# A Mamba scan moved one chunk ahead, and its decays moved to GpSimd

## The chip, the cores and the metric

One Trainium2 chip, one core. The metric is the device time of one execution in microseconds. The engines are TensorE (PE; its weight loads are PEld), VectorE (DVE), ScalarE (ACT), GpSimd (POOL) and SyncE (SP), whose queue issues nearly all DMAs. Each engine takes its instructions in a fixed order.

## The reference

Two layers over 2048 tokens of width 1024: a Mamba-2 mixer and a multi-head latent attention, each behind an RMS norm and with a residual add. The change is in the mixer. Cut to what matters there:

```
proj = h @ w_in;  z, xBC, dt_raw = split(proj)
xBC  = silu(causal_depthwise_conv(xBC, conv_w, conv_b));  xs, Bm, Cm = split(xBC)
dt   = softplus(dt_raw + dt_bias);  A = -exp(A_log)
# per chunk of the sequence, for each of 4 groups (8 heads of 64 channels each):
cum  = cumsum(dt * A)
L    = exp(where(causal, cum[t] - cum[s], -inf))
y    = (C_t . B_s) L dt_s x_s  summed over s
     + exp(cum[t]) C_t . state
state = state * exp(cum[-1]) + sum_s B_s exp(cum[-1] - cum[s]) dt_s x_s
y    = (y + D_skip * x) * silu(z);  y = rms(y over the group) * g_out;  h + y @ w_out
```

## The kernel before

The sequence is cut into four blocks of 512 tokens (`b`) and the mixer's channels into four groups (`g`); `mamba` walks over the sixteen pairs. While the scan of one pair runs, the projections of its neighbours run on TensorE: the output projection `outp` of the pair before, the convolved inputs `xbc` and the gate `zgate` of the next. Each projection is a sweep over k with four PSUM banks (tag `mm`), and each product is three matmuls of high and low halves (L403 to L405). At the end of a sweep the banks are emptied: `hs` on DVE (L1121), `craw` on ACT (L1056, followed by the convolution: L1060 on ACT, three L1062 on DVE, tanh L1064, L1065), `sz` on ACT and DVE (L1091, L1092). In block 0 and 1 the weights are split into halves on ACT and DVE as they come (L434, L437, L442); from block 2 on they are read back already split.

The scan is a Python generator, `ssd(b, g)`, that yields five times per chunk of 128 tokens, four chunks per pair, so 64 chunks in all. `mamba` advances it by one yield for every step or two of the projections; this sets where its instructions stand among theirs. A scheduler orders each engine's instructions by that order of issue, with some shifts where an operand is late. The steps of a chunk:

1. Fetch the chunk's cumulated decays, broadcast to all partitions, into `E` (128 x 8 x 128, tag `big`, two buffers; L1225); transpose B and form C.B on TensorE; split B and C into halves (`Bt`, `Ct`); mask (`CB`); on ACT eight times Relu with a bias per head (L1237) and one exponential (L1238); on DVE multiply by `CB` (L1239).
2. Transpose x (L1244); `Xd` = x dt and `y` = x D on DVE (L1247, L1250); `Xw` = x times the end weight, eight heads on ACT (L1253).
3. Split `Xw` into `Xp` (ACT L1208, POOL L1209); the products of `E` and `Xd` (L1260); the products of `Ct` and the state's halves `Sp` (L410 to L412); add both into `y`.
4. The products of `Bt` and `Xp` (L410 to L412); the state decays and takes them in (L1277, L1278); split the state into `Sp`.
5. Gate `y`, take its power, write it out transposed.

POOL's work in the mixer is the low halves of `Ct`, `Xp` and `Sp` (L1209) and small copies of the convolution's halo (L1055, L1057). `steps(b)` makes `dt`, the cumulated decays and the end weights once per block.

Of the kernel before, what the change touches and what calls it, by code (L numbers as in the profile page):

```python
# [26 lines left out]
G = 4  # L27
# [359 lines left out]
class Net:  # L387
# [492 lines left out]
    def mamba(self, cp):  # L880
        nc = self.nc
        self.state = [None] * G
        self.xn, self.xT, self.dtv, self.conv, self.sz, self.yT, self.rr, self.hs = {}, {}, {}, {}, {}, {}, {}, {}
# [6 lines left out]
        for n, (b, g) in enumerate(items):  # L890
# [34 lines left out]
            scan, done, step = self.ssd(b, g), 0, 0  # L925
# [202 lines left out]
    def steps(self, b):  # L1128
# [9 lines left out]
        wk = self.t(self.sp, "big", [P, D], bufs=2)  # L1138
# [7 lines left out]
        raw, e, q, p, dA, cT = (wk[:, n * P:n * P + P] for n in range(6))  # L1146
# [38 lines left out]
        v.tensor_tensor(wend, wend, dt, ALU.mult)  # L1185
# [6 lines left out]
    def ssd(self, b, g):  # L1192
# [3 lines left out]
        BT, CT, *xs = self.conv.pop((b, g))  # L1196
        szs = self.sz.pop((b, g))
# [3 lines left out]
        def v8(x):  # L1201
            return x.rearrange("p (h d) -> p h d", h=8)

        def pair(tag, n, bufs):
            return self.t(self.sp, tag, [P, 2, n], F32R, bufs=bufs)

        def halves(u, x):
            act(u[:, 0], x, AF.Copy)  # L1208
            nc.gpsimd.tensor_tensor(u[:, 1], x, u[:, 0].bitcast(F32), ALU.subtract)  # L1209
            return u  # L1210

        if b:
            old = halves(pair("Sp", TB, 1), self.state[g])
        for c in range(4):
            s = slice(c * P, (c + 1) * P)
            h0 = c * H + g * 8

            def heads(x):
# [5 lines left out]
            E = self.t(self.sp, "big", [P, D], bufs=2).rearrange("p (h t) -> p h t", h=8)  # L1224
            nc.sync.dma_start(E.rearrange("p h t -> p (h t)"),  # L1225
                              cumT[h0:h0 + 8, :].rearrange("h t -> (h t)").partition_broadcast(P))
            pb = self.t(self.pp, "tr", [P, TB], bufs=4)
            nc.tensor.transpose(pb[:, 0:P], BT[:, s], self.ident)
            nc.tensor.matmul(pb[:, P:2 * P], BT[:, s], CT[:, s], start=True, stop=True)
            Bt = pair("Bt", P, 2)  # L1230
            self.split(Bt[:, 0], Bt[:, 1], pb[:, 0:P])
            if not first:
                Ct = halves(pair("Ct", P, 2), CT[:, s])
            CB = self.t(self.sp, "CB", [P, P], bufs=2)
            v.tensor_tensor(CB, pb[:, P:2 * P], self.triu, ALU.mult)
            for h in range(8):
                act(E[:, h, :], E[:, h, :], AF.Relu, bias=ncum[:, h0 + h:h0 + h + 1])  # L1237
            act(E, E, AF.Exp, scale=-1.0)  # L1238
            v.tensor_tensor(E, E, CB.unsqueeze(1).to_broadcast([P, 8, P]), ALU.mult)  # L1239
            yield  # L1240

            px = self.t(self.pp, "tr", [P, TB], bufs=4)
            for j in range(4):
                nc.tensor.transpose(px[:, j * P:(j + 1) * P], xs[j][:, s], self.ident)  # L1244
            Xd, Xw = self.t(self.sp, "Xd", [P, TB], bufs=2), self.t(self.sp, "Xw", [P, TB], bufs=1)
            with self.tc.high_priority(20):
                v.tensor_tensor(v8(Xd), v8(px), heads(dt), ALU.mult)  # L1247
            y = self.t(self.sp, "y", [P, TB], bufs=2)
            skip = self.Dsk[:, g * 8:g * 8 + 8].unsqueeze(2).to_broadcast([P, 8, 64])
            v.tensor_tensor(v8(y), v8(px), skip, ALU.mult)  # L1250
            for h in range(8):
                hc = slice(h * 64, (h + 1) * 64)
                act(Xw[:, hc], px[:, hc], AF.Copy, scale=wend[:, h0 + h:h0 + h + 1])  # L1253
            yield
            Xp = halves(pair("Xp", TB, 1), Xw)
# [5 lines left out]
            v.tensor_tensor(y, y, yi, ALU.add)  # L1261
            if not first:
                pi = self.t(self.pp, "tr", [P, TB], bufs=4)
                self.late3(pi, Ct[:, 0], Ct[:, 1], old[:, 0], old[:, 1])
                t = self.t(self.sp, "yt", [P, TB], bufs=2)
                v.tensor_tensor(v8(t), v8(pi), heads(ecum), ALU.mult)
                v.tensor_tensor(y, y, t, ALU.add)
            yield
            if not last:
                pst = self.t(self.pp, "tr", [P, TB], bufs=4)  # L1270
                self.late3(pst, Bt[:, 0], Bt[:, 1], Xp[:, 0], Xp[:, 1])
                if first:
                    st = self.state[g] = self.t(self.sp, f"st{g}", [P, TB], bufs=1)
                    v.tensor_copy(st, pst)
                else:
                    st = self.state[g]
                    v.tensor_tensor(v8(st), v8(st), heads(dec), ALU.mult)  # L1277
                    v.tensor_tensor(st, st, pst, ALU.add)  # L1278
                if c < 3:
                    old = halves(pair("Sp", TB, 1), st)  # L1280
# [35 lines left out]
        self.rr[b, g] = rr  # L1316

# [668 lines left out]
```

## Time and profile before

| | |
|---|---|
| Median of 3 runs | 2924.01 us (2920.55 to 2924.09) |
| Profiled execution | 2919.59 us, span 2917.8 us |
| Busy over the span | PE 96%, PEld 56%, DVE 75%, ACT 64%, POOL 34% |
| Mean granted TensorE clock | 0.993 |
| DMA | 507.56 MB, mean 174 GB/s |

In the profile, a group of instructions is named by its line in the kernel, its engine, and out<-in by the names of the tiles. "PE tr L1260 <- DVE big L1239: 10.1, 6, 2.2" says that TensorE's instructions of line 1260 waited for DVE's of line 1239 that write `big`, 10.1 us in all, six times, 2.2 us at most. In a row of groups the last number is the idle time of the engine in front of these instructions, with what ended it. The ends of matmuls are modelled; what can be read of them is the distance between their starts.

### The profile page before, as it was taken

Reading aid. Unit: us, or ns where it says so; the run is one execution under the profiler, and the core shown is the slowest. Engines: PE = TensorE matmul, PEld = TensorE weight load, DVE = VectorE, ACT = ScalarE, POOL = GpSimd, SP = SyncE. Lnnn points to the kernel's source line nnn. Section 1 sums busy time; section 2 is a strip of 40 time slices with the busy share of each in tenths; the row PEclk is TensorE's granted clock in tenths of the full one; section 3 lists DMA queues with packets and bytes.
Section 4 is the critical chain, followed back from the end, with each engine's and each line's share of the span. In section 5 each row is a group of like instructions: output and inputs, shape, how many; then the busy total and the mean of one; then the engine's idle time right before and its main releaser. Section 6 shows DMA issues by size and latency. Waiting matters only on the chain.

```text
span 2917.8 us, 48835 instructions
## 1 busy us (share of the span) xinstructions
PE 2802.7 (96%) x16349; PEld 1648.5 (56%) x16349; DVE 2189.3 (75%) x4757; ACT 1854.4 (64%) x4731; POOL 985.2 (34%) x1200
## 2 busy tenths in 40 slices
PE   7999999998999999999999999999999999999898
PEld 6787755444444444444455455454555555555587
DVE  6778888888877777788776654544888898889476
ACT  7888777666666555666555343432888888888322
POOL 1211112212111221122111212222888888888400
PEclk9999999999999999999999999999999999999899
DMA  5343356665657544476544765556899999999884
GB/s 187 90 120 96 97 167 209 190 186 175 186 157 241 172 127 145 121 223 189 150 140 114 240 200 193 175 171 207 165 183 182 188 187 182 182 188 197 220 265 154
DMA packets 602144, 507.56 MB, mean 174 GB/s; under 512 B 413954, under 2 KB 455938, under 8 KB 601892
## 3 DMA queue, kind: packets, MB, share of 16 engines
q1 hardware_dynamic: 590020, 466.03, 61.3%
q0 software_dynamic: 11872, 38.41, 3.7%
q8 instruction: 128, 2.10, 0.3%
q14 instruction: 124, 1.02, 0.1%
HBM read 303.37 MB, written 104.47 MB: 140 GB/s over the span
## 4 chain that ended last, share of the span: by engine, by line
PE 64%; DVE 14%; ACT 7%; DMA 7%; issue 5%; POOL 2%; SPq 1%; ACTq 0%; POOLq 0%; DVEq 0%
PE mm L403 11%; PE mm L405 11%; PE mm L404 11%; PE tr L403 5%; PE tr L405 5%; PE tr L404 5%; PE mm L1758 4%; DVE cacc L1062 3%; DMA big<-cumT 2%; PE tr L1758 2%; PE mm L1731 2%; DMA wraw<-in_ssm_w_in_dram 2%; PE tr L1731 2%; PE tr L1260 2%; ACT big L1237 1%
## 5 line engine op out<-in xcount | busy, mean ns | idle before, releaser
L1723 POOL TENSOR_TENSOR HL<-Pr,HL 128x512 f16<-128x512 f32 x320 | 370.0, 1156 | 25.6
L403 PE MATMUL mm<-xT,wsp 128*128 128x512 f16 (+1 forms) x800 | 308.4, 385 | 7.4 <-DVE sz L1092 5.3
L404 PE MATMUL mm<-xT,wsp 128*128 128x512 f16 (+1 forms) x800 | 306.1, 383 | 0.0
L405 PE MATMUL mm<-xT,wsp 128*128 128x512 f16 (+1 forms) x800 | 305.2, 383 | 0.6 <-DVE wsp L434 0.5
L1209 POOL TENSOR_TENSOR Xp<-Xw,Xp 128x512 fp32r<-128x512 f32 x64 | 87.2, 1363 | 563.1 <-ACT Xp L1208 536.5
L403 PE MATMUL mm<-wsp,xT 128*128 128x512 f16 (+2 forms) x640 | 233.6, 366 | 1.9 <-ACT craw L1056 1.3
L404 PE MATMUL mm<-wsp,xT 128*128 128x512 f16 (+2 forms) x640 | 232.9, 364 | 1.0 <-DVE wsp L442 1.0
L1717 ACT ACTIVATE Pr<-tr,nm 128x512 f32<-128x512 f32 (+3 forms) x332 | 206.2, 626 | 41.8 <-DVE nm L1712 40.1
L405 PE MATMUL mm<-wsp,xT 128*128 128x512 f16 (+2 forms) x640 | 232.5, 364 | 0.0
L1062 DVE SCALAR_TENSOR_TENSOR cacc<-craw,pack,cacc 128x512 f32<-128x512 f32 x288 | 220.8, 785 | 11.9 <-ACT cacc L1060 10.2
L1722 POOL CAST HL<-Pr 128x512 f16<-128x512 f32 x320 | 195.0, 609 | 91.2 <-ACT Pr L1717 88.7
L1717 ACT ACTIVATE Pr<-mm,nm 128x512 f32<-128x512 f32 (+3 forms) x308 | 191.9, 628 | 44.5 <-DVE nm L1712 38.7
L1706 DVE TENSOR_REDUCE mx<-tr 128x1 f32<-128x512 f32 (+3 forms) x332 | 195.6, 602 | 28.3 <-PE tr L1682 25.9
L403 PE MATMUL mm<-wsp,yT 128*128 128x512 f16 (+1 forms) x512 | 199.4, 389 | 13.3 <-DVE hs L1121 7.2
L1237 ACT ACTIVATE big<-big,d_cum 128x128 f32<-128x128 f32 x512 | 169.8, 391 | 55.4 <-DMA big<-cumT 54.8
L1706 DVE TENSOR_REDUCE mx<-mm 128x1 f32<-128x512 f32 (+3 forms) x308 | 182.1, 604 | 27.6 <-PE mm L1682 20.6
L404 PE MATMUL mm<-wsp,yT 128*128 128x512 f16 (+1 forms) x512 | 197.7, 386 | 0.5 <-DVE wsp L442 0.5
L405 PE MATMUL mm<-wsp,yT 128*128 128x512 f16 (+1 forms) x512 | 197.4, 386 | 0.0
L405 PEld LDWEIGHTS <-xT 128*128 128x128 f16 (+1 forms) x1280 | 124.5, 97 | 117.2 <-issue 2.6
L403 PEld LDWEIGHTS <-xT 128*128 128x128 f16 (+1 forms) x1280 | 125.0, 98 | 106.1 <-issue 14.4
L1253 ACT ACTIVATE Xw<-tr,d_wend 128x64 f32<-128x64 f32 x512 | 111.7, 327 | 111.7 <-DVE y L1250 99.4
L404 PEld LDWEIGHTS <-xT 128*128 128x128 f16 (+1 forms) x1280 | 125.6, 98 | 96.1 <-issue 6.8
(504 smaller groups left out, 7562.3 us busy)
## 6 DMA issues: line engine op xcount, KB each, us to landing
wsp<-w_d SPq DMA_DIRECT2D x68, 512.0 KB, 4.0
wraw<-in_ssm_w_in_dram SPq DMA_DIRECT2D x128, 256.0 KB, 3.4
big<-cumT SPq DMA_DIRECT2D x64, 512.0 KB, 4.2
wraw<-in_ssm_w_out_dram SPq DMA_DIRECT2D x64, 256.0 KB, 3.3
w_d<-wsp SPq DMA_DIRECT2D x32, 512.0 KB, 3.5
wsp<-wo_d SPq DMA_DIRECT2D x32, 512.0 KB, 4.4
st<-w_d SPq DMA_DIRECT2D x56, 256.0 KB, 2.9
wsp<-wu_d SPq DMA_DIRECT2D x28, 512.0 KB, 3.8
```

The source lines that it names most:

```text
L403: mm(out, l_hi, r_hi, start=start, stop=False)
L404: mm(out, l_hi, r_lo, start=False, stop=False)
L405: mm(out, l_lo, r_hi, start=False, stop=stop)
L1062: nc.vector.scalar_tensor_tensor(acc, raw[:, k:k + TB], wk[k], acc, ALU.mult, ALU.add)
L1237: act(E[:, h, :], E[:, h, :], AF.Relu, bias=ncum[:, h0 + h:h0 + h + 1])
L1253: act(Xw[:, hc], px[:, hc], AF.Copy, scale=wend[:, h0 + h:h0 + h + 1])
L1706: v.tensor_reduce(m[:, at:at + 1], s, AX.X, ALU.max, negate=True)
L1717: nc.scalar.activation(tile("Pr", n, j, c)[:, :w], bank("S", n, j, c)[:, :w], AF.Exp, bias=moves[(4 * n + j) % len(moves)], accum_out=sums ...
L1722: nc.gpsimd.tensor_copy(u[:, 0], x)
L1723: nc.gpsimd.tensor_tensor(u[:, 1], x, u[:, 0], ALU.subtract)
L1731: nc.tensor.transpose(bank("T", n, k)[:, j * P:(j + 1) * P], tile("Pr", n, j, k // 4)[:, k % 4 * P:(k % 4 + 1) * P], self.ident)
L1758: nc.tensor.matmul(o, weights, half(n, k, low), start=start, stop=not left[n][at[0]])
```

## The change

The scan is pipelined by one chunk. `ssd` is split: `fetch` issues the DMA of a chunk's decays, `decays` does step 1 of a chunk, `inputs` does step 2 and the split of `Xp`. In the pass over chunk c, `decays` and `inputs` of chunk c + 1 run (of the next pair's first chunk where c is the last), and the fetch for chunk c + 2 goes out after the products of `E` for chunk c.

The engines change too. Adding the bias, the maximum with zero, and the multiply by `CB` run on POOL over the whole 128 x 1024 tile (before: eight Relu on ACT, one multiply on DVE); only the exponential stays on ACT. `Xw` is one POOL op, `Xd` times an end weight that no longer contains dt (before: eight ACT ops from PSUM). The state's decay is a POOL op (before DVE).

The rest follows from the two buffers of `big` being in use all the time: `steps` takes its scratch from `craw` (of three buffers) and reuses two parts of it. `out_power` stands later in block 1's first pair, so that the next pair's inputs exist in time, and the convolution's tiles are released a little later.

```
-            if n == G:
-                parts.append(self.out_power())
...
+                elif n == G:
+                    parts.insert(2, self.out_power())
...
-        wk = self.t(self.sp, "big", [P, D], bufs=2)
+        wk = self.t(self.sp, "craw", [P, TB + 3], bufs=3)
...
-        raw, e, q, p, dA, cT = (wk[:, n * P:n * P + P] for n in range(6))
+        raw, e, q, p = (wk[:, n * P:n * P + P] for n in range(4))
+        dA, cT = e, q
...
-        v.tensor_tensor(wend, wend, dt, ALU.mult)
...
+    def fetch(self, b, g, c):
+        E = self.fetched[b, g, c] = self.t(self.sp, "big", [P, D], bufs=2).rearrange("p (h t) -> p h t", h=8)
+        h0, cumT = c * H + g * 8, self.dtv[b][5]
+        self.nc.sync.dma_start(E.rearrange("p h t -> p (h t)"),
+                               cumT[h0:h0 + 8, :].rearrange("h t -> (h t)").partition_broadcast(P))
+
+    def decays(self, b, g, c):
...
+        E = self.fetched.pop((b, g, c))
+        pb = self.t(self.pp, "tr", [P, TB], bufs=4)
+        nc.tensor.transpose(pb[:, 0:P], BT[:, s], self.ident)
+        nc.tensor.matmul(pb[:, P:2 * P], BT[:, s], CT[:, s], start=True, stop=True)
+        Bt, Ct = self.pair("Bt", P, 2), None
+        self.split(Bt[:, 0], Bt[:, 1], pb[:, 0:P])
+        if b + c:
+            Ct = self.halves(self.pair("Ct", P, 2), CT[:, s])
+        CB = self.t(self.sp, "CB", [P, P], bufs=2)
+        nc.vector.tensor_tensor(CB, pb[:, P:2 * P], self.triu, ALU.mult)
+        nc.gpsimd.tensor_tensor(E, E, ncum[:, h0:h0 + 8].unsqueeze(2).to_broadcast([P, 8, P]), ALU.add)
+        nc.gpsimd.tensor_scalar(E, E, 0.0, None, ALU.max)
+        act(E, E, AF.Exp, scale=-1.0)
+        nc.gpsimd.tensor_tensor(E, E, CB.unsqueeze(1).to_broadcast([P, 8, P]), ALU.mult)
+        self.scan[b, g, c] = [E, Bt, Ct]
+
+    def inputs(self, b, g, c):
...
+        px = self.t(self.pp, "tr", [P, TB], bufs=4)
+        for j in range(4):
+            nc.tensor.transpose(px[:, j * P:(j + 1) * P], xs[j][:, s], self.ident)
+        Xd, Xw = self.t(self.sp, "Xd", [P, TB], bufs=2), self.t(self.sp, "Xw", [P, TB], bufs=1)
+        with self.tc.high_priority(20):
+            v.tensor_tensor(v8(Xd), v8(px), dt[:, h0:h0 + 8].unsqueeze(2).to_broadcast([P, 8, 64]), ALU.mult)
...
+        v.tensor_tensor(v8(y), v8(px), skip, ALU.mult)
+        nc.gpsimd.tensor_tensor(v8(Xw), v8(Xd), wend[:, h0:h0 + 8].unsqueeze(2).to_broadcast([P, 8, 64]), ALU.mult)
+        Xp = self.halves(self.pair("Xp", TB, 1), Xw)
+        self.scan[b, g, c] += [Xd, y, Xp]
...
     def ssd(self, b, g, after):
...
+        if b + g == 0:
+            self.fetch(0, 0, 0)
+            self.fetch(0, 0, 1)
+            self.decays(0, 0, 0)
+            self.inputs(0, 0, 0)
...
         for c in range(4):
+            later = (b, g, c + 1) if c < 3 else after and (*after, 0)
...
+            if later:
+                self.decays(*later)
             yield
+            E, Bt, Ct, Xd, y, Xp = self.scan.pop((b, g, c))
...
+            if c < 2 or after:
+                self.fetch(*((b, g, c + 2) if c < 2 else (*after, c - 2)))
+            yield
...
-                    v.tensor_tensor(v8(st), v8(st), heads(dec), ALU.mult)
+                    nc.gpsimd.tensor_tensor(v8(st), v8(st), heads(dec), ALU.mult)
                     v.tensor_tensor(st, st, pst, ALU.add)
                 if c < 3:
+                    old = self.halves(self.pair("Sp", TB, 1), st)
+            yield
+            if later:
+                self.inputs(*later)
             yield
...
```

More of the change, by code (lines that the diff above doesn't have):

```diff
@@ L882, in mamba @@
         self.state = [None] * G
-        self.xn, self.xT, self.dtv, self.conv, self.sz, self.yT, self.rr, self.hs = {}, {}, {}, {}, {}, {}, {}, {}
+        self.xn, self.xT, self.dtv, self.conv, self.sz, self.yT, self.rr, self.hs, self.scan, self.fetched = ({} for _ in range(10))
         items = [(b, g) for b in range(NB) for g in range(G)]
@@ L924, in mamba @@
                 parts = [self.beside(parts, self.keep2({0: (0, 1, 2), 1: (3, 4, 5), 3: (6, 7)}[g]))]
-            scan, done, step = self.ssd(b, g), 0, 0
+            scan, done, step = self.ssd(b, g, items[n + 1] if n + 1 < len(items) else None), 0, 0
             for part in parts:
@@ new lines, in decays @@
+    def decays(self, b, g, c):
+        nc, act = self.nc, self.nc.scalar.activation
+        dt, ncum, ecum, dec, wend, cumT = self.dtv[b]
+        BT, CT = self.conv[b, g][0:2]
+        s, h0 = slice(c * P, (c + 1) * P), c * H + g * 8
+        E = self.fetched.pop((b, g, c))
[13 more added lines that the diff above has]
+        self.scan[b, g, c] = [E, Bt, Ct]
@@ L1198, in ssd @@
+    def ssd(self, b, g, after):
+        nc, v, act = self.nc, self.nc.vector, self.nc.scalar.activation
+        dt, ncum, ecum, dec, wend, cumT = self.dtv[b]
         ms, e2 = self.t(self.sm, "ms", [P, 4]), self.t(self.sm, "e2y", [P, 4], I32)
@@ L1222, in ssd @@
             last = b == NB - 1 and c == 3
[L1224 to L1239, printed above, removed]
-            yield
[L1242 to L1255, printed above, removed]
+            if later:
+                self.decays(*later)
+            yield
+            E, Bt, Ct, Xd, y, Xp = self.scan.pop((b, g, c))
             yi = self.t(self.pp, "tr", [P, TB], bufs=4)
@@ L1267, in ssd @@
                 v.tensor_tensor(y, y, t, ALU.add)
-            yield
             if not last:
@@ L1316, in ssd @@
         self.rr[b, g] = rr
+        del self.conv[b, g]
     def ev(self, dt=F16):
```

26 lines of the change are left out of this document (14 added, 12 removed).

## The prediction

> **What bounds the kernel now.** I read the busy time by stretches first. The change works inside the Mamba mixer, which fills the first 1,560 us; the columns are busy us (and instructions) of PE, PEld, DVE, ACT and POOL, the granted clock, the DMA share and GB/s. The first four rows are about the four blocks of 512 tokens; the fifth is a stretch of attention.
>
> ```profile
> core 0: us, PE busy (x) PEld busy (x) DVE busy (x) ACT busy (x) POOL busy (x), PEclk, DMA share, GB/s
> 100.00:400.00 300.00, 294.84 (x1702) 228.96 (x1701) 249.10 (x470) 245.96 (x660) 62.28 (x70) 1.00 0.36 110
> 400.00:780.00 380.00, 347.57 (x2007) 182.22 (x2005) 311.98 (x588) 257.34 (x597) 74.74 (x94) 0.98 0.60 187
> 780.00:1160.00 380.00, 359.58 (x2127) 180.73 (x2125) 289.13 (x618) 234.51 (x576) 69.22 (x94) 1.00 0.55 166
> 1160.00:1560.00 400.00, 385.53 (x2369) 197.74 (x2368) 309.29 (x662) 237.26 (x593) 80.29 (x99) 1.00 0.54 161
> 2600.00:2700.00 100.00, 97.86 (x638) 56.76 (x636) 89.57 (x232) 86.80 (x260) 82.78 (x99) 1.00 1.00 198
> ```
>
> TensorE is the bound. All that any rearrangement of other engines can win is its idle time: 5 us in the first block, 32 in the second, 20 and 14 in the last two. DVE is 79 to 83% busy throughout, POOL about 20%. Second view: whom TensorE waited for within the mixer (total us, times, longest).
>
> ```profile
> PE tr L412 <- POOL Xp L1209: 13.6, 18, 1.4
> PE tr L1260 <- DVE big L1239: 10.1, 6, 2.2
> PE tr L1260 <- issue: 9.7, 7, 3.3
> PE mm L403 <- DVE hs L1121: 7.2, 4, 3.3
> PE mm L403 <- ACT craw L1056: 7.1, 9, 1.8
> PE tr L1260 <- DVE Xd L1247: 5.4, 4, 2.3
> PE mm L403 <- DVE sz L1092: 5.3, 5, 1.6
> ```
>
> Two families. The scan's own chain (decays `big`, `Xd`, `Xp` finished just before their products L1260 and L412) costs 13.6 + 10.1 + 9.7 + 5.4 = 38.8 us, if "issue" at L1260 is counted with it. Emptying the projections' banks late (`hs`, `craw`, `sz`) costs 19.6 us. A third view, TensorE in order of time, shows that a long wait is paid twice:
>
> ```profile
> 707.77 0.38 PE L403 MATMUL mm<-wsp,yT 128*128 128x512 f16 x1 [3.28 <-DVE hs L1121]
> ...
> 710.58 0.63 PE L404 MATMUL mm<-wsp,yT 128*128 128x512 f16 x1
> 711.00 0.63 PE L405 MATMUL mm<-wsp,yT 128*128 128x512 f16 x1
> ```
>
> After 3.28 us of idling the products start 0.42 us apart. The 0.98 in the second block's clock column is 380 x 0.02 = 7.6 us of such half speed.
>
> **The change part by part.**
>
> *ACT.* The eight Relu per chunk (L1237) and the eight scalings (L1253) go:
>
> ```profile
> L1237 ACT ACTIVATE big<-big,d_cum 128x128 f32<-128x128 f32 x512 | 169.8, 391 | 55.4 <-DMA big<-cumT 54.8
> L1253 ACT ACTIVATE Xw<-tr,d_wend 128x64 f32<-128x64 f32 x512 | 111.7, 327 | 111.7 <-DVE y L1250 99.4 <-PE tr L1260 5.9 <-DVE rr L507 4.5
> ```
>
> 169.8 + 111.7 = 281 us of work and up to 154 us of in-order waiting in front of them leave ACT, which was busy 975 of 1,460 us. On the path this counts only through the waits above: ACT isn't the bound.
>
> *DVE.* The big multiply (L1239) and the state's decay (L1277) go, 78.1 + 40.7 = 119 us; the end weight's small multiply is under 2 us.
>
> ```profile
> L1062 DVE SCALAR_TENSOR_TENSOR cacc<-craw,pack,cacc 128x512 f32<-128x512 f32 x288 | 220.8, 785 | 11.9 <-ACT cacc L1060 10.2
> ...
> L1239 DVE TENSOR_TENSOR big<-big,CB 128x1024 f32<-128x1024 f32 x64 | 78.1, 1221 | 0.9
> ...
> L1267 DVE TENSOR_TENSOR y<-y,yt 128x512 f32<-128x512 f32 x59 | 56.4, 957 | 0.9
> ...
> L1277 DVE TENSOR_TENSOR st<-st,d_dec 128x512 f32<-128x512 f32 x56 | 40.7, 727 | 42.0 <-POOL Sp L1209 41.9
> L1266 DVE TENSOR_TENSOR yt<-tr,d_ecum 128x512 f32<-128x512 f32 x59 | 40.5, 687 | 7.6 <-PE tr L412 7.6
> L1283 DVE SCALAR_TENSOR_TENSOR y<-y,un,sz 128x512 f32<-128x512 f32 x47 | 39.2, 834 | 0.5
> ```
>
> *POOL.* Per chunk it gains two two-input ops of 1,024 elements, a one-input maximum, the scaled inputs and the state's decay (512 elements each). The nearest rows: its present split of `Ct` (128 elements), one of `Sp` (512) in order of time, the groups of both kinds of 512, and a 512-element cast in attention.
>
> ```profile
> L1209 POOL TENSOR_TENSOR Ct<-BC,Ct x60: 449/464/939, 46.9 to 1534.0; 128x128 fp32r<-128x128 f32 x60
> ```
>
> ```profile
> 1222.70 1.26 POOL L1209 TENSOR_TENSOR Sp<-st,Sp 128x512 fp32r<-128x512 f32 x1 [2.71 <-ACT Sp L1208]
> ```
>
> ```profile
> L1209 POOL TENSOR_TENSOR Xp<-Xw,Xp 128x512 fp32r<-128x512 f32 x63 | 86.0, 1365 | 555.8 <-ACT Xp L1208 529.2 <-PE tr L1260 15.7 <-PE mm L405 10.0
> L1209 POOL TENSOR_TENSOR Sp<-st,Sp 128x512 fp32r<-128x512 f32 x60 | 83.2, 1386 | 165.9 <-ACT Sp L1208 160.0 <-PE mm L405 5.5
> ```
>
> ```profile
> L1722 POOL CAST HL<-Pr 128x512 f16<-128x512 f32 x320 | 195.0, 609 | 91.2 <-ACT Pr L1717 88.7
> ```
>
> From 0.45 at 128 to 1.26 at 512 is 2.1 ns per element on 0.18 us; 1,024 elements give 2.34 us (ends 2.1 and 2.52; the broadcast operand's price is not shown, I take none). The maximum is 2 x 0.609 less a start, 1.04 us. Added: 128 x 2.34 + 64 x 1.04 + (64 + 56) x 1.26 = 518 us, so POOL goes from 287 to about 800 of 1,460 us, 55%, without its waits. It isn't the bound, and the pipelining gives each decay tile a whole chunk (1,560 us / 64, some 24 us) for 5.7 us of POOL and an exponential.
>
> *What POOL's hours cost DVE.* Here the change has its bill. At 1222.70 POOL starts; 0.02 us later DVE starts L1267, which reads two SBUF tensors:
>
> ```profile
> 1222.72 1.79 DVE L1267 TENSOR_TENSOR y<-y,yt 128x512 f32<-128x512 f32 x1
> ```
>
> It takes 1.79 us and ends 0.55 us after POOL's op. Min/median/max of three lines show the kind:
>
> ```profile
> L1062 DVE SCALAR_TENSOR_TENSOR cacc<-craw,pack,cacc x288: 728/747/1786, 37.2 to 1465.1; 128x512 f32<-128x512 f32 x144
> ```
>
> ```profile
> L1267 DVE TENSOR_TENSOR y<-y,yt x60: 677/691/1796, 105.9 to 1562.4; 128x512 f32<-128x512 f32 x60
> ```
>
> ```profile
> L1121 DVE SCALAR_TENSOR_TENSOR hs<-mm,rr,hs x120: 651/745/752, 166.1 to 1540.2; 128x512 f32<-128x512 f32 x120
> ```
>
> Ops with two SBUF inputs are held up to a microsecond; L1121, with one of its two in PSUM, never. Now: L1062 loses 288 x (785 - 747) = 11 us, L1267 59 x (957 - 691) = 16, L1283 and L1277 about 6, so 33 us in four groups. The other two-input groups are about as many ops; between none and the same again (33 to 66) I take 45. Such waiting grows with the sum of squares of POOL's op lengths (longer ops are met more often, and hold longer): now 63 + 60 splits x 1.26² + 60 x 0.45² = 207; added 128 x 2.34² + 64 x 1.04² + 120 x 1.26² = 960. Times 5.6 makes 45 into 252, less a tenth for the two ops that leave DVE: 225, so 180 us more. Lower end, by POOL's busy time alone (800 for 287): about +80; upper, from 66: +270. DVE nets -119 + 180 = +60 us. In the first two blocks, where DVE also splits the weights, I put 55% of the new waits and 27 of 62 chunks: 561 - 52 + 99 = 608 of 680 us, 89%. That is the 89.57 of the attention row, where TensorE kept 97.86; so it can be carried, without slack. The last two come to 598 - 67 + 81 = 612 of 780, 78%.
>
> *Moved steps and queues.* The fetch of a decay tile now is issued behind the products L1260 of the chunk two before. It already starts there:
>
> ```profile
> 1219.92 1.15 PE L1260 MATMUL tr<-Xd,big 128*64 128x64 f32 x32
> ```
>
> ```profile
> 1221.11 0.54 SPq L1225 DMA_DIRECT2D big<-cumT  x1
> ```
>
> Products end at 1221.07, the fetch goes at 1221.11. So SP's order of waiting barely changes and the same 64 transfers go out; no wait on a weights' DMA stands among TensorE's rows above. I take 0 (if weights did queue behind it, up to one landing per chunk in the first chunks that lose their lead). Who waits for the landing is now POOL's add, 54.8 us of waiting leave ACT. On POOL's queue the halo copies (L1055, L1057), the splits of `Ct`, `Sp`, `Xp` now stand behind the decays; L1060 on ACT waits for a halo copy, the exponential for POOL's maximum, and behind both wait ACT's evacuations. I price that below. `out_power` later, dt's scratch in a `craw` buffer and later release of the conv tiles: 0; their cover is slack between blocks; the price without it is a few us four times.
>
> *Sum.* Scan waits 38.8: five go on, for new collisions (the first chunk of the next group needs its conv outputs earlier): -34. Clock: half of 7.6, -4. Evacuation waits 19.6: between +0 (ACT lighter, the 1.2 us multiply no longer in front of `hs`) and three times as much (+40), I take twice, +20, because DVE is fuller. POOL in front of ACT: +3. Together -15 us. The profiled execution took 2919.59 us; minus 15 is 2904.6, and the median run lies 4.4 higher: **2909 us**.
>
> By one page the sum would be another. The Trainium skill's Perfetto Trace Analysis (Optimizing Scalar/DVE Operations) warns that moving work between VectorE and GpSimd may not help, as they share a port; SBUF — State Buffer (Who interferes with whom) says that the later of the two is blocked until the first ends. The 1.79 us row agrees with that; by the first rule taken strictly the DVE gain is nil, and the sum is the first rival's.
>
> **The rivals.** *DVE becomes the bound through POOL (slower).* For it: the net of +60 us, and a first block that has only 5 us to win. Against: ACT's relief, and attention's row. With the upper 270, the first two blocks need 561 - 52 + 148 = 657 of 680; at no more than 90% busy this takes 730, +50. The last two still win about 18: +32 net, 2956. It decides from the point where DVE passes some 92% there (626 us), that is, new waits above 115 us in them.
>
> *The gain is taken back by evacuation (no change).* ACT, in order, stands at an exponential or a halo copy behind a 2.34 us POOL op while a bank is full. 32 conv evacuations losing 0.5 us more each are 16: 2925. For it: the 7.1 us of `craw` now. Against: the 154 us of ACT's waits that go.
>
> *All of it is won.* Scan waits wholly gone, evacuation waits halved, clock back: -39 - 10 - 4 = -53: 2871. For it: 1.2 us less ahead of `hs`; against: DVE's account.
>
> **How the numbers follow.** Forecast (-6 to -30: 2894 to 2918) 0.35; all won 0.19; no change 0.15; DVE bound 0.31. A measurement tells about 0.2%, 6 us, from no change. Faster 0.54, same 0.15, slower 0.31. All won spreads over some 2860 to 2890 and DVE bound over 2930 to 2975; the range leaves 0.08 of the one below and 0.12 of the other above: 2874 to 2952.
>
> **What would show it.** Right: L1260 and L412 leave the list of TensorE's waits (under 8 us together); ACT's busy time in the mixer falls by about 280; POOL's 1,024-element ops take 2.2 to 2.6 us; L1062's mean rises from 785 to about 950, L1121 stays at 745; the first two blocks' DVE share near 89%. Wrong: L403 waiting over 50 us for `hs`, `sz`, `craw` or `wsp`; a POOL op far above 2.5 us; L1260 waiting for POOL's `big`; a first block longer than before.

## The result, and the profile after

The changed kernel takes 3117.9 us (median of four, 3113.76 to 3122.25) against 2924.05 for the kernel before (2920.55 to 2926.63): ratio 1.066, 95% interval 1.064 to 1.069. It is 194 us slower where 15 us of gain were forecast, and far outside the range. The profiled execution's span is 3120.5 us, its mean granted clock 0.969. Here and below, the time of a kernel is the median of its executions in the chip's faster state; max_dve and pipe_pin each had one in the slower state.

All of the loss is in the mixer. Its last scan instruction ends at 1,770 us instead of 1,570; what follows takes 1,351 us instead of 1,348. The busy times of the mixer's stretch, first of before, then of after:

```profile
0.00:1560.00 1560.00, 1472.08 (x8607) 857.18 (x8608) 1225.04 (x2484) 1053.13 (x2622) 298.27 (x380) 0.99 0.52 159
```

```profile
0.00:1760.00 1760.00, 1523.61 (x8620) 886.08 (x8621) 1293.23 (x2361) 803.61 (x1599) 903.27 (x693) 0.95 0.46 141
```

TensorE idles 236 us instead of 88, and its matmuls, the same number, are busy 52 us longer at a clock of 0.95 instead of 0.99: 148 + 52 are the 200 us by which the stretch is longer. DVE's share fell, from 79% to 73%, and ACT's from 68% to 46%. No engine became the bound; the engines wait for one another. TensorE's waits in this stretch (total us, times, longest):

```profile
PE mm L403 <- ACT craw L1056: 82.3, 41, 8.3
PE mm L403 <- DVE sz L1092: 39.5, 10, 7.8
PE mm L403 <- DVE hs L1121: 26.3, 16, 3.5
PE tr L1336 <- DVE y L1318: 23.9, 7, 8.5
PE mm L403 <- ACT xT L441: 10.1, 2, 5.5
```

The waits of the scan's products (38.8 us before) have left the list, as intended; one wait of the scan is new, L1336, which transposes the gated `y` in the first block (23.9 us). Emptying the projections' banks, 19.6 us before, is now 148 us (`craw`, `sz`, `hs`), and the largest part is ACT's. DVE, which empties `hs` and half of `sz`, stands longer for ACT too: its four largest such waits in this stretch (L1323, L442 twice, L434) come to 195 us, where the same rows of before come to 70. What ACT itself waits for in the same stretch:

```profile
ACT big L1225 <- POOL big L1224: 287.1, 56, 15.9
ACT Xp L1196 <- POOL Xw L1248: 112.2, 59, 4.8
ACT xs L1064 <- DVE cacc L1062: 65.0, 31, 7.3
```

The exponential (L1225) stands 287 us for the maximum on POOL (L1224), in 56 of 64 chunks, and the copy of the scaled inputs 112 us for POOL's product. POOL's new groups (busy us, mean ns, idle in front of them and what ended it):

```profile
L1224 POOL TENSOR_SCALAR big<-big 128x1024 f32<-128x1024 f32 x64 | 189.2, 2956 | 3.9
L1226 POOL TENSOR_TENSOR big<-big,CB 128x1024 f32<-128x1024 f32 x64 | 163.8, 2560 | 268.9 <-DVE CB L1222 246.4 <-DVE ri L575 9.8 <-DVE rss L785 7.7
L1223 POOL TENSOR_TENSOR big<-big,d_cum 128x1024 f32<-128x1024 f32 x64 | 131.6, 2056 | 142.5 <-DMA big<-cumT 131.6 <-PE tr L411 6.8 <-PE tr L412 3.6
L1248 POOL TENSOR_TENSOR Xw<-Xd,d_wend 128x512 f32<-128x512 f32 x64 | 73.2, 1143 | 53.4 <-DVE Xd L1244 53.4
L1307 POOL TENSOR_TENSOR st<-st,d_dec 128x512 f32<-128x512 f32 x56 | 64.8, 1157 | 3.1
```

One place in order of time shows how this reaches TensorE (start, duration, engine, line, in brackets the wait in front of it):

```profile
892.87 2.36 POOL L1226 TENSOR_TENSOR big<-big,CB 128x1024 f32<-128x1024 f32 x1
895.78 2.35 POOL L1223 TENSOR_TENSOR big<-big,d_cum 128x1024 f32<-128x1024 f32 x1
898.22 3.08 POOL L1224 TENSOR_SCALAR big<-big 128x1024 f32<-128x1024 f32 x1
901.34 1.06 ACT L1225 ACTIVATE big<-big 128x1024 f32<-128x1024 f32 x1 [6.80 <-POOL big L1224]
...
908.60 0.67 ACT L1056 ACTIVATE craw<-mm,un 128x512 f32<-128x512 f32 x1
...
909.32 0.59 PE L403 MATMUL mm<-wsp,yT 128*128 128x512 f16 x1 [6.75 <-ACT craw L1056]
909.70 0.63 PE L404 MATMUL mm<-wsp,yT 128*128 128x512 f16 x1
...
913.54 0.56 PE L404 MATMUL mm<-wsp,yT 128*128 128x512 f16 x1
913.94 0.38 PE L405 MATMUL mm<-wsp,yT 128*128 128x512 f16 x1
914.15 0.27 PE L1215 MATMUL tr<-pack,BC 128*128 128x128 f32 x1
```

ACT stands 6.80 us at the exponential while POOL adds and takes the maximum. The bank that TensorE needs is emptied further down ACT's queue, at 908.60, and TensorE stands 6.75 us. Then its matmuls start about 0.4 us apart until 913.94, and 0.21 us apart afterwards: 4.6 us at half speed, 2.3 us more lost. The Trainium skill (TensorE: Matmul & The Clock Gate, What's actually happening) says that an idle window of about 3.4 us halves the clock and that about as long a busy stretch restores it. These rows agree as far as they go: one stop of 6.75 us, then 4.6 us at half speed. Where the threshold lies they do not show.

### The profile page after: what moved, and what is told of

The parts are those of the page before. It is cut to its first block, busy times and chain, and to the rows that moved or that the text cites. A ratio compares the mean times of both kernels' runs of the same rounds, so it can differ in the third digit from the quotient of the medians.

```text
span 3120.5 us, 48020 instructions
## 1 busy us (share of the span) xinstructions
PE 2855.1 (91%) x16349; PEld 1676.8 (54%) x16349; DVE 2256.1 (72%) x4633; ACT 1604.9 (51%) x3707; POOL 1590.1 (51%) x1512
## 4 chain that ended last, share of the span: by engine, by line
PE 44%; DVE 10%; POOL 7%; DMA 5%; issue 5%; ACT 3%; SPq 0%; POOLq 0%; ACTq 0%; DVEq 0%
PE mm L403 7%; PE mm L405 6%; PE mm L404 6%; PE tr L403 4%; PE tr L405 4%; PE tr L404 4%; PE mm L1792 4%; DVE cacc L1062 2%; DMA big<-cumT 2%; POOL big L1224 2%; PE tr L1792 2%; PE mm L1765 2%; PE tr L1765 1%; POOL big L1223 1%; POOL Sp L1197 1%
## 5 line engine op out<-in xcount | busy, mean ns | idle before, releaser
L403 PE MATMUL mm<-xT,wsp 128*128 128x512 f16 (+1 forms) x800 | 319.9, 401 | 72.5 <-ACT craw L1056 30.7
L405 PE MATMUL mm<-xT,wsp 128*128 128x512 f16 (+1 forms) x800 | 315.7, 395 | 5.4 <-DVE wsp L442 3.6
L404 PE MATMUL mm<-xT,wsp 128*128 128x512 f16 (+1 forms) x800 | 316.2, 395 | 0.0
L1226 POOL TENSOR_TENSOR big<-big,CB 128x1024 f32<-128x1024 f32 x64 | 163.8, 2560 | 268.9 <-DVE CB L1222 246.4
L1062 DVE SCALAR_TENSOR_TENSOR cacc<-craw,pack,cacc 128x512 f32<-128x512 f32 x288 | 253.6, 904 | 16.6 <-ACT cacc L1060 14.7
L403 PE MATMUL mm<-wsp,yT 128*128 128x512 f16 (+1 forms) x512 | 204.4, 399 | 65.7 <-ACT craw L1056 40.5
L403 PE MATMUL mm<-wsp,xT 128*128 128x512 f16 (+2 forms) x640 | 238.3, 373 | 22.3 <-ACT craw L1056 11.1
L404 PE MATMUL mm<-wsp,xT 128*128 128x512 f16 (+2 forms) x640 | 236.1, 369 | 3.5 <-DVE wsp L442 3.5
L405 PE MATMUL mm<-wsp,xT 128*128 128x512 f16 (+2 forms) x640 | 236.6, 370 | 0.0
L1225 ACT ACTIVATE big<-big 128x1024 f32<-128x1024 f32 x64 | 67.6, 1056 | 300.4 <-POOL big L1224 287.1
L1223 POOL TENSOR_TENSOR big<-big,d_cum 128x1024 f32<-128x1024 f32 x64 | 131.6, 2056 | 142.5 <-DMA big<-cumT 131.6
L404 PE MATMUL mm<-wsp,yT 128*128 128x512 f16 (+1 forms) x512 | 202.6, 396 | 0.0
L405 PE MATMUL mm<-wsp,yT 128*128 128x512 f16 (+1 forms) x512 | 202.0, 395 | 0.0
L1224 POOL TENSOR_SCALAR big<-big 128x1024 f32<-128x1024 f32 x64 | 189.2, 2956 | 3.9
L405 PEld LDWEIGHTS <-xT 128*128 128x128 f16 (+1 forms) x1280 | 124.7, 97 | 120.6 <-issue 6.3
L404 PEld LDWEIGHTS <-xT 128*128 128x128 f16 (+1 forms) x1280 | 125.8, 98 | 110.6 <-issue 22.6
```

What stands on the lines that cost most here:

```text
L403: mm(out, l_hi, r_hi, start=start, stop=False)
L404: mm(out, l_hi, r_lo, start=False, stop=False)
L405: mm(out, l_lo, r_hi, start=False, stop=stop)
L1062: nc.vector.scalar_tensor_tensor(acc, raw[:, k:k + TB], wk[k], acc, ALU.mult, ALU.add)
L1223: nc.gpsimd.tensor_tensor(E, E, ncum[:, h0:h0 + 8].unsqueeze(2).to_broadcast([P, 8, P]), ALU.add)
L1224: nc.gpsimd.tensor_scalar(E, E, 0.0, None, ALU.max)
```

## The experiments

The runs were to tell apart where 194 us come from. Theory A: ACT, in order, stands for POOL's chain and the banks behind it stay full. B: DVE loses time to the shared port whenever POOL works. C: the order itself. D: the maximum's price. E: POOL's own queue grows long, and what stands behind in it comes late. In the table, "idle" is TensorE's idle time up to the last scan instruction, summed over the gaps between matmuls from the first one on (the stretch above also counts some 14 us ahead of it); "stands" is ACT's wait in front of the work on the decays, with the engine or transfer that ended it; "held" is DVE's time above the median of each group of instructions, which is how I sum port waits; all in us. Each kernel's ratio was measured against the kernel before on the same chip.

| kernel | time | ratio (95%) | idle | stands | POOL busy | held |
|---|---|---|---|---|---|---|
| before | 2924 | 1 | 74 | 55 DMA | 305 | 47 |
| pipe_only | 2933 | 1.003 (1.002 to 1.004) | 89 | 100 DMA | 321 | 41 |
| relu_mulv | 2927 | 1.002 (1.000 to 1.003) | 77 | 117 DMA | 458 | 74 |
| act_relu | 2971 | 1.017 (1.014 to 1.019) | 111 | 135 DMA | 605 | 151 |
| relu_touch | 2987 | 1.022 (1.020 to 1.023) | 120 | 130 POOL | 624 | 141 |
| relu_dummy | 3016 | 1.032 (1.030 to 1.034) | 144 | 124 DMA | 949 | 162 |
| relu_once | 3029 | 1.037 (1.034 to 1.040) | 158 | 191 POOL | 738 | 200 |
| max_dve | 3045 | 1.042 (1.039 to 1.045) | 169 | 138 DVE | 746 | 202 |
| mul_back | 3095 | 1.059 (1.057 to 1.061) | 206 | 333 POOL | 763 | 137 |
| after | 3118 | 1.066 (1.064 to 1.069) | 223 | 287 POOL | 915 | 221 |
| engines_only | 3139 | 1.074 (1.071 to 1.077) | 235 | 166 POOL | 924 | 229 |
| late_exp | 3142 | 1.075 (1.072 to 1.079) | 235 | 2 POOL | 922 | 219 |
| touch_behind | 3205 | 1.097 (1.094 to 1.100) | 282 | 367 POOL | 938 | 147 |

**The order alone** (pipe_only) and **the engines alone** (engines_only).

```
pipe_only: after, with Relu x8 + Exp and Xw x8 on ACT, mask multiply and state's decay on DVE
engines_only: before, with add, max, mask multiply, Xw and state's decay on nc.gpsimd
```

> The new order alone: the scan lies a chunk behind and the decays are fetched a chunk ahead, while the Relu and the exponential stay on ScalarE, the mask multiply and the state's decay on VectorE, the scaled inputs on ScalarE, as before the change. Theory A (ScalarE, which works its queue in order, stands at the exponential behind GpSimd's chain while filled banks wait to be emptied): the wait of the scan's matmul goes (38.8 us of the kernel before) and nothing takes its place: 2880 to 2905 us. Theory B (VectorE loses the time to the shared port whenever GpSimd works, 175 us more of it after the change): GpSimd's added hours are gone, so 2880 to 2905 as well. Theory C (the order itself costs: the scan's matmuls and copies fall where they hold up the projections): 2950 us or more, most of the 194 us lost remaining.

> The engine moves alone, in the order of the kernel before: Relu as an add and a maximum on GpSimd, mask multiply, scaled inputs and state's decay on GpSimd, the scan in its own chunk. Theory A: the exponential now waits for GpSimd without a chunk of slack, so 3050 us or more, with waits of the exponential over 250 us. Theory B: the same hours of GpSimd, so the same port waits, 3050 to 3120. Theory C: the order of before keeps the time near before, 2924 to 2950.

2933.0 and 3138.7 us, the second above B's window as well as C's. The engine moves cost 215 us in the old order, and the new order takes about 20 of them away; theory C falls as the cause of the loss. (The exponential stands 166 us in engines_only, not the 250 that theory A named; the rest shows as TensorE waiting 74 us for the masked decays.) But pipe_only misses every expectation: the order wins nothing. TensorE's waits in pipe_only:

```profile
PE mm L403 <- ACT craw L1056: 18.9, 20, 2.6
PE mm L403 <- DVE sz L1092: 12.1, 7, 3.3
PE mm L403 <- DVE hs L1121: 11.7, 9, 1.8
PE mm L404 <- DVE wsp L442: 9.7, 4, 7.4
PE mm L403 <- ACT xT L441: 6.6, 2, 5.3
```

L1260's successor is gone from the list, and the waits for banks and weights have grown by about as much: `craw`, `sz` and `hs` alone from 19.6 to 42.7 us.

**The Relu back on ACT** (act_relu) and **the exponential later** (late_exp).

```
act_relu:
-        nc.gpsimd.tensor_tensor(E, E, ncum..., ALU.add)
-        nc.gpsimd.tensor_scalar(E, E, 0.0, None, ALU.max)
+        for h in range(8): act(E[:, h, :], E[:, h, :], AF.Relu, bias=ncum[...])
late_exp: Exp behind the copy of Xp(c + 1) on ACT, the mask multiply behind its low half on POOL
```

> The changed kernel with one thing undone: the Relu back on ScalarE (eight instructions with the bias), so that no add and no maximum run on GpSimd and the exponential waits for nothing of GpSimd's. GpSimd keeps the mask multiply, the scaled inputs and the state's decay (about 300 of the 623 us of the four groups). Theory A: the exponential's wait of 287 us and with it the waits of TensorE for the evacuations are gone: 2880 to 2930 us. Theory B: about half of the port waits stay: about 3000 to 3030. Theory C: near 3100.

> The changed kernel with all its work on the same engines, but the exponential issued later on ScalarE (behind the copy of the next chunk's scaled inputs' high half) and GpSimd's mask multiply behind the low half of the same inputs, so that ScalarE reaches the exponential later and stands there less. Theory A: the wait of the exponential falls by more than half and TensorE's waits for the evacuations with it: 2930 to 3010 us. Theories B and C: the same hours of GpSimd and the same order of the scan, so 3100 to 3130.

act_relu takes 2971.3 us: the add and the maximum, for eight Relu, are 147 of the 194 us. That is neither A's 2930 nor B's 3000. late_exp takes 3142.4, against theory A as I had put it, and 12 us above the window of B and C. Its exponential no longer stands, but ACT and TensorE stand for POOL elsewhere:

```profile
ACT Xp L1196 <- POOL Xw L1259: 173.5, 59, 8.4
PE mm L403 <- ACT craw L1056: 79.4, 39, 7.6
PE mm L403 <- DVE sz L1092: 43.3, 13, 6.6
PE tr L1301 <- POOL big L1237: 39.2, 9, 7.5
```

The later multiply makes the scan's products wait for `big`, these release the buffer later, so the next fetch lands later; POOL, whose queue holds `Xw` behind the add, now waits 357 us for that fetch (131.6 in after). So I read it; in any case issuing the exponential later moved the standing, it did not remove it.

**Where the standing sits.** max_dve, relu_once and mul_back each take one operation off POOL; pipe_late moves the decays behind the state's update; pipe_dummy lets POOL work for nobody.

```
max_dve:    nc.gpsimd.tensor_scalar(E, E, 0.0, None, ALU.max)  ->  nc.vector
relu_once:  the same line  ->  act(E, E, AF.Relu)
mul_back:   nc.gpsimd.tensor_tensor(E, E, CB..., ALU.mult)     ->  nc.vector
pipe_late:  pipe_only, self.decays(*later) moved from the chunk's top to ahead of self.inputs(*later)
pipe_dummy: pipe_only + 32 nc.gpsimd ops of 128x128 per chunk on a scratch tile
```

> The changed kernel with the maximum alone moved, from GpSimd (2.96 us each, 64 of them) to VectorE. The exponential still waits for another engine's chain (add on GpSimd, maximum on VectorE). Theory A (what counts is that ScalarE's queue stands for a chain on other engines): the chain is two thirds as long, 3020 to 3070 us. Theory B (port): a third of GpSimd's hours goes: 3050 to 3070. Theory D (the price of the maximum, three times what the sum took, is what makes GpSimd late): 2970 to 3000, as with the Relu on ScalarE.

> The changed kernel with the maximum replaced by one Relu of 128x1024 on ScalarE, ahead of the exponential: GpSimd's add stays, its maximum goes, ScalarE works 1.06 us more per chunk and still waits for the add. Theory A: ScalarE stands for the add alone (1.9 us instead of 5): 2990 to 3040 us. Theory B: 3050 to 3070. Theory D: 2970 to 3000.

> The changed kernel with the mask multiply alone back on VectorE: the add, the maximum, the scaled inputs and the state's decay stay on GpSimd, which no longer stands for the mask (246 us of its waits). Theory A: the exponential still waits for an add and a maximum, 3060 to 3100 us. Theory B: a quarter of GpSimd's added hours goes, about 3070. Theory E: GpSimd's queue is 2.4 us per chunk shorter and stands less, so the add and the maximum are ready sooner: 3000 to 3050.

3044.9, 3029.5 and 3094.5 us. max_dve and mul_back land in A's windows, relu_once too; D falls as put, since taking the maximum away still leaves 58 us over act_relu; but the maximum is a large part of the 147, as the two kernels without it on POOL are 73 and 88 us faster than the changed one. B named 3050 to 3070, or about 3070, for the three: max_dve lies just below, the other two outside. mul_back is the telling one: DVE is held 137 us, less than act_relu's 151, and yet it is 123 us slower. Its row of ACT's waits:

```profile
ACT big L1225 <- POOL big L1224: 333.3, 63, 15.4
```

> The new order alone with the decays of the next chunk issued late: behind the state's update and ahead of the next chunk's inputs, instead of ahead of this chunk's scan. In the order alone ScalarE stands 100 us for the fetched decays, because the work on them begins some 6 us after their fetch. If that standing is what gave back the scan's waits, it goes and the time is 2895 to 2920 us; if TensorE's idle time only changes its place (ScalarE and VectorE empty the banks no sooner), 2925 to 2940.

> The new order alone (2933 us as measured), and beside it GpSimd works on a scratch tile that nobody else reads: per chunk 8 multiplies by a broadcast, 8 maxima, 8 multiplies behind the decays and 8 multiplies behind the inputs, each 128x128, about as many elements as the five operations that the change gives GpSimd. No engine waits for these instructions, but they share VectorE's port and stand in GpSimd's queue. Theory A (other engines stand in their queues behind GpSimd's chain): 2930 to 2955 us. Theory B (VectorE loses the time to the port while GpSimd works, whoever waits for GpSimd): 3050 to 3120, most of the 185 us between this order alone and the changed kernel.

pipe_late takes 2976.6 us, slower than either expectation; ACT still stands 80 us for the fetched decays. pipe_dummy takes 3688.9 and answers another question than the one put. Its 32 operations took 0.46 to 0.56 us each, 16 us per chunk where the changed kernel's five take 9.7, and stood in POOL's queue in long bunches ahead of the low halves (TensorE's waits, in the first 1,580 of the 2,338 us that its mixer takes):

```profile
PE tr L412 <- POOL Xp L1200: 169.7, 11, 60.7
PE tr L412 <- POOL Sp L1200: 100.4, 2, 70.6
```

It shows what POOL's queue can cost (756 us over pipe_only), and that DVE, held 66 us beside 1,317 us of POOL, was not what paid for it.

**Hours without a wait** (relu_dummy; POOL's hours are its working time). Now with six operations of 128x256, which stand in POOL's queue where the add and the maximum stand; the first of them waits for `CB`, not for the fetch.

```
act_relu +
+        for h in range(3): nc.gpsimd.tensor_tensor(F, F, CB..., ALU.mult)     # F: [P, 2, P] bf16
+        for h in range(3): nc.gpsimd.tensor_scalar(F, F, 0.0, None, ALU.max)
```

> The kernel with the Relu back on ScalarE (2971 us as measured), and in GpSimd's queue, where the changed kernel has the add and the maximum (behind the mask multiply, ahead of the low halves and the scaled inputs), three multiplies and three maxima of 128x256 on a scratch tile of bfloat16 that nobody else reads: some 4.6 us per chunk, as the add and the maximum together. GpSimd has the hours and the queue of the changed kernel, but the exponential waits for none of it. Theory A (ScalarE's queue stands for GpSimd's chain, filled banks with it): 2970 to 3000 us. Theory B (the shared port: VectorE loses by GpSimd's hours whoever waits): 3080 to 3130. Theory E (GpSimd's own queue: the scaled inputs and the low halves behind the long operations come late): 3020 to 3080.

3016.1 us, 4 below E's window and 16 above A's; B's lies far off. The dummies took 354 us, more than the add and the maximum (321):

```profile
L1229 POOL TENSOR_SCALAR idle<-idle 128x256 bf16<-128x256 bf16 x192 | 185.5, 966 | 15.6
L1227 POOL TENSOR_TENSOR idle<-idle,CB 128x256 bf16<-128x256 bf16 x192 | 168.7, 878 | 277.1 <-DVE CB L1224 260.0 <-DVE rsy L789 7.5 <-DVE ri L575 4.9
```

So POOL's hours in their place cost 45 us, and 102 of the 147 are not in them. DVE is held only 11 us longer than in act_relu, and ACT's copy waits longer for `Xw` (128.5 us for 89.4). So I take it that the 45 us go through POOL's queue.

**Place, length, and both** (relu_touch, touch_behind).

```
relu_touch:   act_relu +
+        nc.gpsimd.tensor_scalar(E[:, :, 0:1], E[:, :, 0:1], 0.0, None, ALU.add)    # ahead of the Relu
touch_behind: act_relu +
+        three multiplies of F by parts of E and three maxima on F, then the line above behind them
```

> The kernel with the Relu on ScalarE (2971 us), plus one GpSimd instruction on 8 elements per partition of the fetched decays (adding zero) that the Relu has to wait for. It stands in GpSimd's queue where the add and the maximum of the changed kernel stand, directly behind the mask multiply, and takes almost no time. So ScalarE depends on GpSimd's queue as in the changed kernel, without the 4.9 us of work. Theory A1 (what costs is the place in GpSimd's queue, which stands for the mask while ScalarE stands for it): 3020 to 3075 us. Theory A2 (what costs is the length of the add and the maximum that ScalarE stands for): 2970 to 2990. Theories B and E (GpSimd's hours and its queue's length): 2970 to 2985.

> The two effects put together without the add and the maximum: the Relu is on ScalarE, GpSimd does three multiplies and three maxima of 128x256 on the scratch tile (the multiplies read the fetched decays, so they wait for the landing as the add did), and then the tiny instruction on the decays for which the Relu waits. GpSimd's hours, their place and what ScalarE stands for are those of the changed kernel; only who does the Relu differs. Theory A2 (ScalarE stands for the length of what GpSimd does ahead of it): 3080 to 3150 us, and a wait of ScalarE for GpSimd ahead of the Relu of 250 us or more. If the two measured effects only add up (45 for the hours, 15 for the place in the queue), 3025 to 3040, and something in the add and the maximum themselves is left to find.

relu_touch takes 2986.5 us, 15 over act_relu: a wait for POOL's queue costs little where ACT stood for the fetch anyway (130 us for POOL, 135 for the fetch). touch_behind takes 3204.7, more than A2 expected, and far above the 3031 that the two effects add up to:

```profile
ACT big L1233 <- POOL big L1231: 367.0, 61, 16.0
PE mm L403 <- ACT craw L1058: 93.3, 37, 7.8
PE mm L403 <- DVE sz L1094: 49.2, 10, 7.2
PE mm L403 <- DVE hs L1123: 36.0, 21, 4.5
```

A1 falls with the first, simple addition with the second. The pair relu_dummy and touch_behind tells the rest. POOL's hours are alike (949 and 938 us), DVE is held no more (162 and 147), and each engine does the same work but for one tiny POOL operation per chunk; the difference is that in one ACT waits for the dummies' end, and POOL, in front of them, for the fetch. Together that is worth 189 us, and DVE's four largest waits for ACT grow with it, from 152 to 299 us. POOL waits for the fetch as long in relu_touch (143 us in each), where it costs no more than the 15. That it passes the changed kernel fits ACT's eight Relu still standing behind that wait, but no run took them away.

**What takes the order's gain back** (short_before, short_pipe, pipe_pin).

```
short_*:  for k in range(1, 4)  ->  range(3, 4)     # two of three L1062 per bank left out, in both orders
pipe_pin: pipe_only, Relu and Exp of chunk c + 1 behind the copy of Xp(c + 1) on ACT
```

> The kernel before with two of the three VectorE steps of the convolution (192 instructions of about 0.78 us, 150 us) left out, so that VectorE, which is busy 82 to 89% of the mixer's time, has room. It is the reference for the next run: 2880 to 2924 us.

> The same two steps left out of the new order alone. The scan's waits of 38.8 us are gone in that order, and yet it is 9 us slower than before. Theory F (VectorE's work per chunk, nearly full, gives the gain back as late banks): with room on VectorE this kernel is 20 to 40 us faster than the one before with the same steps left out. Theory G (the order itself costs as much as the waits were worth, whoever has room): within 10 us of it or slower.

> The new order alone (2933 us), with the Relu and the exponential of the next chunk put behind the copy of its scaled inputs in ScalarE's queue; all else, the mask and the splits too, stays early. ScalarE stands 100 us for the fetched decays in the order alone, 55 before. If that standing gave back the scan's waits (theory F2), it shrinks to under 30 us and the time is 2890 to 2920. If the gain is lost whatever ScalarE stands for (theory G), 2925 to 2960.

2890.1 (ratio 0.990, 0.987 to 0.992) and 2898.9 us (0.992, 0.990 to 0.993): both orders win 34 us from the room on DVE, and the new one stays 9 behind. pipe_pin takes 2955.2 (1.011, 1.009 to 1.013), although ACT's standing for the fetch is gone from its list of waits. F and F2 fall, G holds; why the order returns what it wins stays open.

**The cheap moves** (before_st, relu_mulv, before_xwst).

```
before_st:   before, v.tensor_tensor(v8(st), ..., heads(dec), ALU.mult)  ->  nc.gpsimd
relu_mulv:   act_relu, mask multiply on nc.vector
before_xwst: before_st + Xw as one nc.gpsimd multiply of Xd
```

> The kernel before with one edit, the state's decay on GpSimd (64 us of GpSimd's time, 41 us off VectorE's, which waited 42 us for GpSimd ahead of it). No wait of ScalarE is added. Theory A: nothing that empties a bank stands for GpSimd, so 2905 to 2930. Theory B or E: GpSimd's hours cost about 0.13 to 0.47 us for each us, so 2932 to 2955.

> The new order with only the scaled inputs and the state's decay on GpSimd (Relu and exponential on ScalarE, mask multiply on VectorE): 137 us of GpSimd's added time instead of 300. ScalarE's copy of the scaled inputs still waits for GpSimd. Theory A: the wait of that copy is what the kernel with the Relu on ScalarE lost (38 us over the order alone), so 2955 to 2975. Theory B or E: the loss goes with the hours, so half of 38: about 2950.

> The kernel before with the state's decay and the scaled inputs on GpSimd, in the old order. ScalarE is rid of eight scalings per chunk (112 us, and 99 us of standing for VectorE), but its copy of the scaled inputs stands for GpSimd. If a short GpSimd operation in front of ScalarE is free (theory A2: the new order with these two moves was 6 us faster than without), 2905 to 2919 us; if the old order's scan then waits for the scaled inputs, 2925 to 2950.

before_st takes 2919.3 us, ratio 0.998 (0.997 to 0.999): the one kernel with the whole computation that is faster than both, by the least that can be told. relu_mulv takes 2927.0, less than any theory gave it; its interval overlaps pipe_only's, so that `Xw` and the state's decay cost nothing in the new order, and the 44 us up to act_relu are the mask multiply. DVE's held time rises by 77 us and TensorE's idle time by 34 with it; whether port or queue is to blame for this one was not separated. before_xwst, at 2945.5 (1.008, 1.006 to 1.009), lies in the second of its windows, but not for the reason given there: TensorE's wait for `Xp` at L412 falls from 14.0 us in before_st to 0.6. It is ACT's copy that stands for `Xw`; without the chunk of slack the move costs 26 us over before_st:

```profile
ACT Xp L1207 <- POOL Xw L1250: 141.7, 51, 7.3
```

So the 194 us are: the order 9, the mask multiply 44 with the two small moves -6, the add and the maximum 147. Of these, 45 are POOL's hours and queue, 15 the place in it, and some 87 are left, which I put down to what appears only when ACT stands for the length of POOL's work. The 87 are a difference and were not measured alone; the pair above shows that such a surplus exists (3205 against the 3031 of the sum).

## Why the prediction was wrong, point by point

*"POOL in front of ACT: +3" and the evacuation waits.* This is the step that failed. The mechanism stood in the text as the rival "the gain is taken back by evacuation": ACT stands at an exponential behind a POOL operation while a bank is full. I priced it as 32 evacuations losing 0.5 us, 16 us. Measured, the exponential stands in 56 of 64 chunks for 5.1 us, not for one operation but for two and the multiply ahead of them, and the evacuation waits, which I let grow by 20 to some 40 us, are 148 us: L403 waiting over 50 us for banks was a sign of being wrong that the prediction named. I set "154 us of ACT's waits that go" against it and did not put the new wait in their place. The chunk of slack that I named as cover for POOL's chain did not cover it: the exponential stands in ACT's queue ahead of the evacuations, wherever the scan's next use is.

*Durations.* The 1,024-element multiply took 2.34 us at the least, as worked out. The maximum took 2.96 instead of 1.04: a cast of 512 elements in attention was no measure for it. The add, with its operand broadcast along the inner elements, was cheaper than I had it (1.89 at the least), and `Xw` and the decay too (1.14 and 1.16 for 1.26). POOL's added work came to 623 us instead of 518.

*The port.* DVE is held 221 us instead of 47, +174 where I had +180. Ops with two SBUF inputs pay it (the means of L1062 and L1065 were 785 and 699 ns before), the one with an input in PSUM does not:

```profile
L1062 DVE SCALAR_TENSOR_TENSOR cacc<-craw,pack,cacc 128x512 f32<-128x512 f32 x288 | 253.6, 904 | 16.6 <-ACT cacc L1060 14.7 <-POOL craw L1055 0.6
L1121 DVE SCALAR_TENSOR_TENSOR hs<-mm,rr,hs 128x512 f32<-128x512 f32 x120 | 85.9, 740 | 6.8 <-PE mm L405 6.7
L1065 DVE SCALAR_TENSOR_TENSOR BC<-BC,cacc 128x512 f32<-128x512 f32 x32 | 32.1, 1002 | 5.6 <-ACT BC L1064 5.6
```

That the size was met is in part luck. Summed over the traces, the squares of the lengths of all of POOL's tensor operations in the mixer go from 265 to 1,684 us², and the prediction's rule would give 270 to 300 us for them. The maximum makes up 561 of the 1,684 where the prediction counted 69, but it held DVE little: max_dve and relu_once, without it on POOL, are held 202 and 200 us. With the two-input operations alone the rule comes close: 265, 444, 871 and 1,123 us² in before, relu_mulv, act_relu and after, for 47, 74, 151 and 221 us held. In pipe_dummy it does not (655 us², 66 us).

The conclusion (a DVE 89% busy in the first two blocks) was wrong, and so was the rival built on it: from 100 to 880 us, about those two blocks, DVE is 78% busy. Its share in the four stretches of before is 76 to 83%, not 79 to 83. And mul_back, act_relu and touch_behind are held alike (137 to 151 us) with 3095, 2971 and 3205 us. The Trainium skill's SBUF — State Buffer (Who interferes with whom) says that a VectorE instruction with two SBUF inputs contends with a GpSimd instruction that reads SBUF. The rows above agree for the single operation, but it did not set the time of this kernel. The warning of the Trainium skill's Perfetto Trace Analysis (Optimizing Scalar/DVE Operations), that offloading between the two might not help because they share a port, points the right way; but these runs leave the port little beyond the mask multiply's 44 us and what POOL's hours cost.

*The scan's waits, -34.* They went, and pipe_only shows that nothing was won: +9. TensorE's idle time came back at the banks. This term was wrong by 43 us on its own.

*The clock, -4.* It followed the waits the other way: 0.95 instead of 0.99 in the mixer, some 52 us.

*SP's queue, 0.* The transfers themselves did not stand among TensorE's waits, but the fetch has little lead: POOL's add waits 131.6 us for its landing, where ACT waited 54.8.

## What to carry to other kernels

Before moving work to another engine, ask which queue will stand for its result, and what else is in that queue: an in-order engine that empties PSUM banks pays for the whole chain in front of its one dependent instruction. Price that wait as the chain's length times the number of chunks, not as a chance collision, and add the clock that TensorE loses after each stop. A wait that leaves the list is a gain only if the idle time falls with it; here a pipelining removed 39 us of waits and the idle time grew by 15.

## What the runs showed of the hardware that was not expected

On GpSimd a one-input maximum over 128x1024 f32 took 2.76 to 3.23 us, longer than a two-input multiply of that shape (2.56 us mean), while VectorE did the same maximum in 0.94 us in the mean and 0.69 in the median (max_dve). The multiply with an operand broadcast along the outer axis took 2.34 us at the least, the add with one broadcast along the inner axis 1.89. A quarter of the elements, in bfloat16, took a third of the time and more: 0.88 us (multiply) and 0.97 us (maximum) for 128x256. These short operations hardly held VectorE: 354 us of them added 11 us, where the mask multiplies of 128x1024 in f32, some 163 us, added 77. The type need not be the reason: in pipe_dummy, 1,023 us of f32 operations of 128x128 added 25 us to pipe_only's.
